# How the transposed operand of two large products leaves PSUM: split straight from PSUM, or scaled into SBUF first and split there

## The chip, the cores and the metric

The kernel runs on one core of a Trainium2 chip. The time is that of the device for one execution, in microseconds (us), as a median of repeated runs. The engines have the profile's names: PE multiplies and transposes, DVE and ACT work element by element, POOL does little here, and SP issues most of the transfers (DMA).

## What is computed

One layer of a streaming encoder with 256 tokens of width 4096, batch 1, all in fp32:

```python
xn = rms_norm(x, norm_in_g)
q, k, v, z_a, a_c, g_c, z_c = split(xn @ w_in)            # 4096 x 14336
y_a = rms_norm(chunked_attention(q, k, v, rel_table), attn_out_g) * silu(z_a)
y_c = rms_norm(conv_module(a_c, g_c, ...), conv_out_g) * silu(z_c)
h = x + concatenate([y_a, y_c]) @ w_out                    # 4096 x 4096, "the projection"
gate = sigmoid(rms_norm(h, ple_norm_g) @ w_ple_gate + b_ple_gate)   # 4096 x 4096, "the last gate"
h = h + gate * (p @ w_ple)                                 # 256 x 4096
return rms_norm(h, final_g)
```

## The kernel before

**Products.** Every fp32 product is made of three products of a shorter fp32 form (fp32r): each operand is split into a high part (the value rounded to that form) and a low part (the value minus its high part), and PE adds high·high, low·high and high·low. Weights come as blocks of 128 rows by 2 × 512 columns (tile `wt`, five buffers, loaded by SP at L440); ACT casts the high part (`wh`, L204) and DVE subtracts to get the low part (`wl`, L205), three buffers each.

**Pairs.** `mixed_product` takes the 32 blocks of 128 rows of the inner dimension in 16 pairs. A plain pair is 24 matmuls into four accumulator banks. A combined pair is 21 matmuls, by a scheme of seven products instead of eight: for it, DVE makes sums of the weights (`ua`, `ub`, L467 to L475) and sums of the other operand (`comb`), and four more PSUM banks hold partial results (`acc_P`). The order of the pairs is a string; the two products of the change begin with the order `late`, the eight odd pairs plain, and then 0 (combined), 2, 4 (combined) and so on.

**The operand.** `operand(src, g, c, ...)` makes chunk c, that is 512 of the 4096 inner rows (four blocks of 128), of the transposed left operand: PE transposes the activations into PSUM, 2 blocks to a bank (L170), and each block is scaled by a vector `g` on its way out. `split_from_psum` does that per block of 128 × 256: ACT writes the scaled high part (L156), and DVE reads PSUM again, scales and subtracts the high part (L157). For the combined pairs `combine` takes the first two blocks of a chunk: ACT writes the first block, scaled, into a row of SBUF (L284), DVE makes four sums of 128 columns in a second row, two of them reading the second block from PSUM (L268 to L271), and these 512 columns are split by ACT and DVE (L276, L277). The operand of the projection is `yT` (eight chunks, the last not combined here but later, by `combine_again`), that of the last gate `hT` (eight chunks, all combined). `y_ahead` and `h_ahead` call it one chunk ahead of the pair that uses it: chunks 0 and 1 at the last pair of the product before, then one for each odd pair. An odd pair uses the last two blocks of its chunk. After the eighth chunk of `hT`, `embedding` loads the layer's input embedding `p` into the tile `pin` (SP, L1113) and transposes it on PE.

**Buffers and order.** The rows of `combine`, the tile `pin` and the loaded rows of the gate's bias (L1002) share three buffers with the tag "row". PSUM has eight banks, four for accumulators (`acc`) and four for the rest. When one product ends and the next begins, the next takes over the accumulators as DVE empties them (L1067 for the gated columns before the projection, L1151 for h before the last gate). No order is written out by hand around the change: a list scheduler puts the instructions of the loops into each engine's queue, and each queue is worked through in order, SP's too.

Of the kernel before, what the change touches and what calls it, by code (L numbers as in the profile page):

```python
# [10 lines left out]
F32 = mybir.dt.float32  # L11
F32R = mybir.dt.float32r
AF = mybir.ActivationFunctionType
ALU = mybir.AluOpType
AX = mybir.AxisListType

P = 128
NB = 512
# [7 lines left out]
def hybrid_block(  # L26
# [23 lines left out]
    nc = tc.nc  # L50
    _, T, D = x.shape
# [16 lines left out]
    def pool(name, bufs, stack=ctx, side=0, **kw):  # L68
        return stack.enter_context(tc.tile_pool(name=name, bufs=bufs, side=sides[side], **kw))
# [12 lines left out]
    spool = pool("spool", 2, first_scratch, 1)  # L82
# [3 lines left out]
    def tmp_psum():  # L86
        return ps_tmp.tile([P, 512], F32, tag="tmp", name="tmp_ps")
# [61 lines left out]
    def big_tile(pool=None):  # L149
        return (pool or big).tile([P, 4, 2, T], F32R, tag="big", name="big_t")  # L150

    def split_from_psum(dst, i, src, scale):

        hi, lo = dst[:, i, 0, :], dst[:, i, 1, :]
        return (
            nc.scalar.activation(hi, src, AF.Identity, scale=scale),  # L156
            nc.vector.scalar_tensor_tensor(  # L157
                lo, src, scale, hi.bitcast(F32), ALU.mult, ALU.subtract
            ),
        )  # L160
# [3 lines left out]
    def transposed(src, blocks, then=lambda ins: None):  # L164

        pt = tmp_psum()
        for i, b in enumerate(blocks):
            for h in range(NH):
                last_transpose[:] = [
                    nc.tensor.transpose(  # L170
                        pt[:, i * T + h * P : i * T + (h + 1) * P],
                        src[:, h, b] if len(src.shape) == 4 else src[:, h, b * P : (b + 1) * P],
                        ident,
                    )
                ]
                then(*last_transpose)
        return [pt[:, i * T : (i + 1) * T] for i in range(len(blocks))]
# [80 lines left out]
    def sum_rows():  # L258
        return [spool.tile([P, NB], F32, tag="row", name="comb", bufs=3) for _ in range(2)]

    def combined_parts(dst, at, s, a, a01, a11, g, then=lambda ins: None):

        a00, a10 = a[:, :P], a[:, P:]
        s3, s5, s2, s4 = (s[:, i * P : (i + 1) * P] for i in range(4))
        stt = nc.vector.scalar_tensor_tensor
        then(nc.vector.tensor_tensor(s3, a00, a10, ALU.subtract))  # L268
        then(stt(s5, a11, g, a10, ALU.mult, ALU.subtract))
        then(stt(s2, s5, -1.0, a00, ALU.mult, ALU.subtract))  # L270
        then(stt(s4, a01, g, s2, ALU.mult, ALU.add))  # L271

        def split():
            hi, lo = dst[:, at : at + 2, 0, :], dst[:, at : at + 2, 1, :]
            src = s.rearrange("q (i t) -> q i t", t=T)
            then(nc.scalar.copy(hi, src))  # L276
            then(nc.vector.tensor_tensor(lo, src, hi.bitcast(F32), ALU.subtract))  # L277

        return split

    def combine(dst, at, pts, g):

        a, s = sum_rows()
        nc.scalar.activation(a[:, :T], pts[0], AF.Identity, scale=g[:, :1])  # L284
        combined_parts(dst, at, s, a[:, :T], pts[1][:, :P], pts[1][:, P:], g[:, 1:2])()

    def combine_again(dst, at, t, i, rows, then=lambda ins: None):

        a, s = rows
        then(  # L290
            nc.vector.tensor_tensor(
                a.rearrange("q (i t) -> q i t", t=T), t[:, i : i + 2, 0, :].bitcast(F32),
                t[:, i : i + 2, 1, :].bitcast(F32), ALU.add,
            )
        )
        return combined_parts(dst, at, s, a[:, :T], a[:, T : T + P], a[:, T + P :], 1.0, then)

    def comb_tile(combs, n_kept=0):

        if len(combs) < D // NB // 2 - 1 + n_kept:  # L300
            combs.append(big_tile(more))
        else:
            combs.append(keep.tile([P, 4, 2, T], F32R, tag="comb", name="comb_t"))

    def operand(src, g, c, tiles, combs, pool=None, combined=True):

        t = big_tile(pool)
        if c % 2 == 0:
            comb_tile(combs)
        for pair in range(2):  # L310
            blocks = (2 * pair, 2 * pair + 1)
            pts = transposed(src, blocks)
            for b, pt in zip(blocks, pts):
                split_from_psum(t, b, pt, g[:, b : b + 1])
            if pair == 0 and combined:
                combine(combs[c // 2], 2 * (c % 2), pts, g[:, :2])
        tiles.append(t)

    def pair_parts(src):
# [186 lines left out]
    tt, stt = nc.vector.tensor_tensor, nc.vector.scalar_tensor_tensor  # L506
# [53 lines left out]
    for c in range(0, 4, 2):  # L560
        if c:
            t = upool.tile([P, 4, 2, T], F32R, tag="big", name="big_t", bufs=1)
        else:
            t = keep.tile([P, 4, 2, T], F32R, tag="comb", name="comb_t")
# [3 lines left out]
    def combinations(c, then=lambda ins: None):  # L568

        rest = []  # L570

        def begin():
            rows = spool.tile([P, 2, NB], F32, tag="stage", name="comb")
            rest.append(
                combine_again(*xS[2 * c], xT[c], 0, (rows[:, 0], rows[:, 1]), then)
            )

        return begin, lambda: rest.pop()()

    def first_pairs(add):  # L580
# [62 lines left out]
        for n in range(1, n_x + 1):  # L643
# [26 lines left out]
    rows = [(conv_ln_g, KCW), (conv_ln_b, KCW), (b_dw, KCW), (attn_out_g, AW // P),  # L670
            (conv_out_g, KCW), (ple_norm_g, KD)]
    n_rows = sum(n for _, n in rows)
    at = [sum(n for _, n in rows[:i]) for i in range(len(rows))]
# [324 lines left out]
    def broadcast_row(src, n0, n, **kw):  # L998

        kw = kw or dict(tag="row", bufs=3)  # L1000
        t = spool.tile([P, n], F32, name="row", **kw)
        nc.sync.dma_start(  # L1002
            t, bass.AP(tensor=src.tensor, offset=src.offset + n0, ap=[[0, P], [1, n]])
        )
        return t
# [5 lines left out]
    for c in range(2):  # L1011
        uC[2 * c] = act.tile([P, 2, 2, T], F32R, tag="act", name="comb_u"), 0
        scratch = spool.tile([P, 2, NB], F32, tag="stage", name="comb")
        combine_again(*uC[2 * c], uS[c], 0, (scratch[:, 0], scratch[:, 1]))()
    first_scratch.close()
    spool = upool = pool("lpool", 2, side=1)
    y_c = []
    ssq_c = cpool.tile([P, NH, CW // NB], F32, name="ssq_c")
    for c0, order in zip(range(0, CW // NB, 2), point):
        row = broadcast_row(b_pw, c0 * NB, 2 * NB, tag="stage")  # L1020
        rows = [row[:, j * NB : (j + 1) * NB] for j in range(2)]
# [29 lines left out]
    for c in range(2, D // NB):  # L1051
        if c % 2 == 0:
            comb_tile(xS, 1)
        combine_again(xS[c // 2], 2 * (c % 2), xT[c], 0, sum_rows())()
# [24 lines left out]
    def y_ahead(pair):  # L1079
        while len(yT) < min(pair // 2 + 2, D // NB):  # L1080
            c = len(yT)
            if c == D // NB - 2:
                fill(len(later))
            y, g, at = (y_a[c], ga, 4 * c) if c < len(y_a) else (y_c[c - len(y_a)], gc, 4 * (c - len(y_a)))
            operand(
                y, g[:, at : at + 4], c, yT, yS, None if c else more, combined=c < D // NB - 1
            )
        if pair == late[9][0]:

            rest = []  # L1090
            later.append(
                lambda: rest.append(combine_again(yS[-1], 2, yT[-1], 0, sum_rows()))
            )
            later.append(lambda: rest.pop()())
# [23 lines left out]
    def h_ahead(pair):  # L1118
        while len(hT) < min(pair // 2 + 2, D // NB):
            c = len(hT)  # L1120
            operand(hs[c], gp[:, 4 * c : 4 * c + 4], c, hT, hS)
            if len(hT) == D // NB:
                embedding()

    ssq_h = cpool.tile([P, NH, D // NB], F32, name="ssq_h")
    for c0 in range(0, D // NB, 2):
        for j in range(2):
            hc = act.tile([P, NH, NB], F32, tag="act", name="hc")
            c = c0 + j
# [85 lines left out]
    rows, fgs = [], []  # L1215
# [51 lines left out]
    def sum_of(h, at):  # L1267
        s = end[:, 0, h : h + 1]
        pin(nc.vector.tensor_reduce(s, ssq_f[:, h, :at], AX.X, ALU.add))
        return s  # L1270
# [45 lines left out]
    s = sum_of(1, n_f + 1)  # L1316
# [35 lines left out]
```

## Time and profile before

| | |
|---|---|
| median of three runs | 2029.14 us (2028.86 to 2029.4) |
| profiled execution | 2028.23 us, span 2026.5 us |
| granted TensorE clock, mean | 0.998 |
| the projection's odd pairs (operand `yT`) | about 1307 to 1368 us of the span |
| the last gate's odd pairs (operand `hT`) | about 1644 to 1706 us of the span |

The profile is one execution. A row of a group gives the source line, the engine, the operation and its tiles, the number of instructions, their busy time in us, the mean of one in ns, and after the second bar the idle time of the engine just ahead of them with what ended it. A row of a timeline begins with the start and the duration in us. PEld is PE's weight load, which runs beside its matmuls; a wait of PE for an operand shows there. The name in front of the arrow is what is written.

### The profile page before, as it was taken

How to read it: one execution, taken by the hardware profiler on the slowest of the kernel's cores; microseconds unless marked ns; L12 is line 12 of the kernel's file. 1: busy time of each engine (PE TensorE's matmuls, PEld its weight loads, DVE VectorE, ACT ScalarE, POOL GpSimd, SP SyncE). 2: the span in 40 equal slices, each digit the busy share in tenths (PEclk: the TensorE clock that was granted, in tenths of full speed). 3: DMA queues.
4: the chain of work that ended last, by engine and by line, in shares of the span. 5: the costliest groups of instructions: out<-in, count | busy, mean ns of one | idle time of the engine just before them, and what ended most of it. 6: DMA issues, size and time to landing. Idle time of an engine off the chain costs nothing.

```text
span 2026.5 us, 26195 instructions
## 1 busy us (share of the span) xinstructions
PE 2010.8 (99%) x9073; PEld 1654.4 (82%) x9073; DVE 1903.4 (94%) x2708; ACT 1215.0 (60%) x1583; POOL 46.9 (2%) x50
## 2 busy tenths in 40 slices
PE   9999999999999999999999999999999999999997
PEld 7888888888888888788888888888888888888876
DVE  7999999889999997888899999999999999999998
ACT  7655545655655555776556556666665666655555
POOL 0000000000000000000000000000000000000000
PEclk9999999999999999999999999999999999999999
DMA  8787878678678867456666666676666656666765
GB/s 295 222 238 234 255 217 250 177 247 240 188 221 246 252 198 241 156 177 209 196 208 207 208 204 211 208 239 210 203 211 197 208 194 201 208 218 207 231 207 180
DMA packets 171168, 436.70 MB, mean 215 GB/s; under 512 B 13966, under 2 KB 17182, under 8 KB 171034
## 3 DMA queue, kind: packets, MB, share of 16 engines
q1 hardware_dynamic: 161952, 417.93, 63.9%
q0 software_dynamic: 8432, 16.25, 4.8%
q8 instruction: 71, 1.16, 0.2%
q10 hardware_dynamic: 650, 0.84, 0.1%
q14 instruction: 63, 0.52, 0.1%
HBM read 430.77 MB, written 4.19 MB: 215 GB/s over the span
## 4 chain that ended last, share of the span: by engine, by line
PE 95%; DVE 3%; issue 1%; ACT 1%; DMA 0%; POOLq 0%; POOL 0%; ACTq 0%; SPq 0%; DVEq 0%
PE acc L385 73%; PE acc_P L385 17%; PE tmp_ps L170 1%; DVE cv L724 1%; PE acc L229 1%; DVE wl L205 1%; PE tmp_ps L893 0%; PE tmp_ps L877 0%; PE tmp_ps L911 0%; PE tmp_ps L916 0%; PE acc L373 0%; ACT wh L204 0%; PE tmp_ps L892 0%; DVE ul L205 0%; DMA xin<-in_x_dram 0%
## 5 line engine op out<-in xcount | busy, mean ns | idle before, releaser
L385 PE MATMUL acc<-wh,big_t 128*128 128x512 f32 x4154 | 1283.3, 391 | 0.6 <-DVE y_c L1043 0.4
L204 ACT CAST wh<-wt 128x1024 fp32r<-128x1024 f32 (+1 forms) x737 | 710.1, 974 | 523.3 <-PE acc L385 364.3
L385 PEld LDWEIGHTS acc<-wh,big_t 128*128 128x128 f32 x4154 | 777.0, 188 | 160.8 <-DVE y_c L1043 0.9
L205 DVE TENSOR_TENSOR wl<-wt,wh 128x1024 fp32r<-128x1024 f32 (+1 forms) x737 | 817.4, 1122 | 39.9 <-ACT wh L204 33.6
L385 PE MATMUL acc<-wl,big_t 128*128 128x512 f32 x2077 | 801.9, 391 | 0.1
L385 PEld LDWEIGHTS acc<-wl,big_t 128*128 128x128 f32 x2077 | 389.5, 188 | 82.5 <-DVE wl L205 1.8
L204 ACT CAST uh<-ua 128x1024 fp32r<-128x1024 f32 x174 | 182.9, 1052 | 91.1 <-DVE ua L468 46.3
L205 DVE TENSOR_TENSOR ul<-ua,uh 128x1024 fp32r<-128x1024 f32 x174 | 212.0, 1219 | 9.6 <-ACT uh L204 8.1
L724 DVE SCALAR_TENSOR_TENSOR cv<-uT,dw,cv 128x250 f32<-128x250 f32 (+19 forms) x480 | 203.6, 464 | 1.1
L385 PE MATMUL acc_P<-uh,big_t 128*128 128x512 f32 x528 | 161.8, 392 | 0.0
L204 ACT CAST uh<-ub 128x1024 fp32r<-128x1024 f32 x92 | 96.8, 1052 | 95.5 <-DVE ub L475 79.2
L205 DVE TENSOR_TENSOR ul<-ub,uh 128x1024 fp32r<-128x1024 f32 x92 | 112.2, 1220 | 6.7 <-ACT uh L204 5.6
L385 PEld LDWEIGHTS acc_P<-uh,big_t 128*128 128x128 f32 x528 | 98.0, 188 | 23.2 <-ACT uh L204 3.7
L385 PE MATMUL acc_P<-ul,big_t 128*128 128x512 f32 x264 | 101.3, 392 | 0.0
L467 DVE TENSOR_TENSOR ua<-wt 128x512 f32<-128x512 f32 x102 | 69.9, 685 | 17.3 <-DMA wt<-in_w_in_dram 10.7
L385 PE MATMUL acc<-uh,big_t 128*128 128x512 f32 x266 | 82.5, 390 | 0.0
L385 PE MATMUL acc_P<-wh,big_t 128*128 128x512 f32 x266 | 82.1, 389 | 0.0
L468 DVE TENSOR_TENSOR ua<-wt 128x512 f32<-128x512 f32 x102 | 69.6, 683 | 4.3 <-DMA wt<-in_w_in_dram 3.6
L385 PE MATMUL acc_P<-uh,comb_t 128*128 128x512 f32 x228 | 70.1, 390 | 0.1
L475 DVE TENSOR_TENSOR ub<-ub,wt 128x512 f32<-128x512 f32 x92 | 63.0, 685 | 0.8
L474 DVE TENSOR_TENSOR ub<-ua,wt 128x512 f32<-128x512 f32 x92 | 62.9, 683 | 0.3
L385 PEld LDWEIGHTS acc_P<-ul,big_t 128*128 128x128 f32 x264 | 49.3, 188 | 12.5 <-DVE ul L205 2.0
(243 smaller groups left out, 1485.5 us busy)
## 6 DMA issues: line engine op xcount, KB each, us to landing
wt<-in_w_in_dram SPq DMA_DIRECT2D x416, 512.0 KB, 4.5
wt<-in_w_out_dram SPq DMA_DIRECT2D x128, 512.0 KB, 4.3
wt<-in_w_ple_gate_dram SPq DMA_DIRECT2D x128, 512.0 KB, 4.2
wt<-in_w_pw_dram SPq DMA_DIRECT2D x32, 512.0 KB, 4.8
ua<-in_w_in_dram SPq DMA_DIRECT2D x31, 512.0 KB, 4.3
ua<-in_w_in_dram POOLq DMA_DIRECT2D x31, 512.0 KB, 8.7
wt<-in_w_in_dram SPq DMA_DIRECT2D x31, 256.0 KB, 2.8
hc<-in_x_dram SPq DMA_DIRECT2D x8, 512.0 KB, 4.7
```

The source lines that it names most:

```text
L170: nc.tensor.transpose(pt[:, i * T + h * P : i * T + (h + 1) * P], src[:, h, b] if len(src.shape) == 4 else src[:, h, b * P : (b + 1) * P], ...
L204: nc.scalar.copy(wh[:, :kc, :], wt[:, :kc, :]),
L205: nc.vector.tensor_tensor(wl[:, :kc, :], wt[:, :kc, :], wh[:, :kc, :].bitcast(F32), ALU.subtract),
L229: nc.tensor.matmul(acc, a, b[:, k, :], start=kb == 0 and kind == 0, stop=kb == kblocks - 1 and kind == 2,)
L385: nc.tensor.matmul(banks[name], a, b, start=name not in begun, stop=final and ends[name] == n and kind == 2 and not (left and name in "P2 ...
L467: plus(ua[:, 0], w0[:, 0], w0[:, 1])
L468: plus(ua[:, 1], w0[:, 1], w1[:, 1])
L474: plus(ub[:, 0], ua[:, 0], w1[:, 1])
L475: plus(ub[:, 1], ub[:, 0], w1[:, 0])
L724: nc.vector.scalar_tensor_tensor(cv[:, i, PAD - k :], uT[:, i, : T + k - PAD], dw[:, b, k : k + 1], cv[:, i, PAD - k :], ALU.mult, ALU.add,)
```

## The change

`operand` now copies each transposed block, scaled by ACT, from PSUM into a row of fp32 in SBUF, two blocks to a row of 512 columns. Then one ACT cast of 512 columns makes both high parts, and one DVE subtraction of 512 columns, from SBUF, both low parts. `combine` takes its four quarters from that row, so its own copy L284 is gone and none of its sums reads PSUM or scales. A combined chunk therefore takes three rows of the tag "row" where it took two, and one that is not combined takes two where it took none. `combine_again` passes quarters too. The embedding still uses `split_from_psum`. The orders of the pairs and their products are the same.

```diff
     def sum_rows():
         return [spool.tile([P, NB], F32, tag="row", name="comb", bufs=3) for _ in range(2)]
 
-    def combined_parts(dst, at, s, a, a01, a11, g, then=lambda ins: None):
-        a00, a10 = a[:, :P], a[:, P:]
+    def combined_parts(dst, at, s, a00, a10, a01, a11, then=lambda ins: None):
         s3, s5, s2, s4 = (s[:, i * P : (i + 1) * P] for i in range(4))
         stt = nc.vector.scalar_tensor_tensor
         then(nc.vector.tensor_tensor(s3, a00, a10, ALU.subtract))
-        then(stt(s5, a11, g, a10, ALU.mult, ALU.subtract))
+        then(nc.vector.tensor_tensor(s5, a11, a10, ALU.subtract))
         then(stt(s2, s5, -1.0, a00, ALU.mult, ALU.subtract))
-        then(stt(s4, a01, g, s2, ALU.mult, ALU.add))
+        then(nc.vector.tensor_tensor(s4, a01, s2, ALU.add))
...
-    def combine(dst, at, pts, g):
-        a, s = sum_rows()
-        nc.scalar.activation(a[:, :T], pts[0], AF.Identity, scale=g[:, :1])
-        combined_parts(dst, at, s, a[:, :T], pts[1][:, :P], pts[1][:, P:], g[:, 1:2])()
+    def combine(dst, at, a):
+        s = spool.tile([P, NB], F32, tag="row", name="comb", bufs=3)
+        (a00, a10), (a01, a11) = ((a[:, i, :P], a[:, i, P:]) for i in range(2))
+        combined_parts(dst, at, s, a00, a10, a01, a11)()
...
-        return combined_parts(dst, at, s, a[:, :T], a[:, T : T + P], a[:, T + P :], 1.0, then)
+        return combined_parts(dst, at, s, *(a[:, i * P : (i + 1) * P] for i in range(4)), then)
...
     def operand(src, g, c, tiles, combs, pool=None, combined=True):
         t = big_tile(pool)
         if c % 2 == 0:
             comb_tile(combs)
+        rows = sum_rows()
         for pair in range(2):
             blocks = (2 * pair, 2 * pair + 1)
-            pts = transposed(src, blocks)
-            for b, pt in zip(blocks, pts):
-                split_from_psum(t, b, pt, g[:, b : b + 1])
+            a = rows[pair].rearrange("q (i t) -> q i t", t=T)
+            for i, pt in enumerate(transposed(src, blocks)):
+                b = blocks[i]
+                nc.scalar.activation(a[:, i], pt, AF.Identity, scale=g[:, b : b + 1])
+            hi, lo = (t[:, 2 * pair : 2 * pair + 2, q, :] for q in range(2))
+            nc.scalar.copy(hi, a)
+            nc.vector.tensor_tensor(lo, a, hi.bitcast(F32), ALU.subtract)
             if pair == 0 and combined:
-                combine(combs[c // 2], 2 * (c % 2), pts, g[:, :2])
+                combine(combs[c // 2], 2 * (c % 2), a)
         tiles.append(t)
```

In the changed file the copies are L315, the cast of a row L317, the low part of a row L318; the sums of `combined_parts` are L267 to L270 and its split L275 and L276; `combine_again` adds at L290; matmuls are L389, weight loads L444, the sums of weights L471 to L479, the emptying of accumulators L1071 and L1155, the row loads L1006 and the load of `pin` L1117.

## The prediction

> **What bounds the kernel now.** I read the page first (busy time, then the chain that ended last), then the windows of the two stages in which the changed routine runs, then the waits of PE's weight loads after them. The columns of the page's first line are busy us, share of the span and instructions; those of a window are its length, then busy us of PE, PEld, DVE, ACT and POOL with instruction counts, the granted clock, the DMA share and GB/s.
>
> ```profile
> PE 2010.8 (99%) x9073; PEld 1654.4 (82%) x9073; DVE 1903.4 (94%) x2708; ACT 1215.0 (60%) x1583; POOL 46.9 (2%) x50
> PE 95%; DVE 3%; issue 1%; ACT 1%; DMA 0%; POOLq 0%; POOL 0%; ACTq 0%; SPq 0%; DVEq 0%
> 1300.00:1370.00 70.00, 70.00 (x342) 58.42 (x341) 64.59 (x115) 46.85 (x76) 0.00 (x0) 1.00 0.70 232
> 1640.00:1710.00 70.00, 70.00 (x344) 58.58 (x343) 66.22 (x121) 48.98 (x85) 0.69 (x1) 1.00 0.59 191
> PEld acc_P L385 <- ACT uh L204: 4.5, 16, 0.5
> PEld acc_P L385 <- DVE ul L205: 1.3, 6, 0.3
> PEld acc L385 <- DVE wl L205: 0.9, 3, 0.3
> PEld acc L373 <- DVE big_t L205: 0.5, 1, 0.5
> ```
>
> PE carries 95% of the chain. In both windows of the change it is busy for all 70 us at clock 1.00: **there is no wait of PE there to remove**, so a lighter DVE or a heavier ACT is worth nothing unless PE is made to wait, and every such wait is lost for good. The last four rows are all the waits of PE's loads from 1720 to 2000 us, 7.2 us in sum; only from there could a gain come.
>
> **The routine itself.** Groups by line: count, busy us, mean ns, idle before and its releaser.
>
> ```profile
> L156 ACT ACTIVATE big_t<-tmp_ps,prm 128x256 fp32r<-128x256 f32 x64 | 27.7, 470 | 4.1 <-DVE big_t L157 2.5 <-PE tmp_ps L170 1.6
> L157 DVE SCALAR_TENSOR_TENSOR big_t<-tmp_ps,prm,big_t 128x256 fp32r<-128x256 f32 x64 | 28.2, 476 | 0.0
> L276 ACT CAST big_t<-comb 128x512 fp32r<-128x512 f32 x20 | 12.0, 615 | 2.6 <-DVE comb L271 2.2 <-issue 0.3
> L277 DVE TENSOR_TENSOR big_t<-comb,big_t 128x512 fp32r<-128x512 f32 x20 | 13.5, 686 | 1.6 <-ACT big_t L276 1.6
> L284 ACT ACTIVATE comb<-tmp_ps,prm 128x256 f32<-128x256 f32 x15 | 7.1, 470 | 0.0
> L268 DVE TENSOR_TENSOR comb<-comb 128x128 f32<-128x128 f32 x30 | 8.6, 287 | 0.9 <-ACT comb L284 0.7
> L269 DVE SCALAR_TENSOR_TENSOR comb<-tmp_ps,prm,comb 128x128 f32<-128x128 f32 x15 | 5.2, 343 | 0.0
> L270 DVE SCALAR_TENSOR_TENSOR comb<-comb 128x128 f32<-128x128 f32 x30 | 8.5, 284 | 0.1
> L271 DVE SCALAR_TENSOR_TENSOR comb<-tmp_ps,prm,comb 128x128 f32<-128x128 f32 x15 | 5.2, 344 | 0.0
> L205 DVE TENSOR_TENSOR wl<-wt,wh 128x1024 fp32r<-128x1024 f32 (+1 forms) x737 | 817.4, 1122 | 39.9 <-ACT wh L204 33.6
> ```
>
> A combined chunk on ACT: before 4 × 470 + 470 + 615 = 2965 ns. After: the four copies still read PSUM in 256 columns (470 each, the nearest row for the new output type), the extra copy L284 goes, two casts of 512 columns come (615 each): 1880 + 1230 + 615 = 3725 ns, **+0.76 us**. On DVE: before 4 × 476 + 287 + 343 + 284 + 344 + 686 = 3848 ns. After: two subtractions of 512 columns (686, the row of the same form), and four sums of 128 columns all from SBUF (287, 287, 284, 287): 1372 + 1145 + 686 = 3203 ns, **−0.645 us**. The page's fifteen combined chunks (x15) make ACT +11.4 and DVE −9.7 us; the one that is not combined adds 1230 ns on ACT and takes 532 on DVE. ACT has some 21 of 70 us idle in each window and DVE 4 to 5, so neither sum reaches PE. In `combine_again` one form replaces another at the same 287 against 286 to 290: nothing. PE's and POOL's instructions are the same in number. So the price lies only in order and buffers, at five places.
>
> **First, the start of the projection.** PE, from the last matmuls of the previous product (acc_10871) into the new one (acc_11620 on), before and after:
>
> ```order
> L385 MATMUL acc_10871<-wh,big_t 128x512 x2
> L385 MATMUL acc_10871<-wl,big_t 128x512
> L385 MATMUL acc_11620<-wh,big_t 128x512 x2
> L385 MATMUL acc_11620<-wl,big_t 128x512
> L385 MATMUL acc_11620<-wh,big_t 128x512 x2
> L170 MATMUL tmp_ps<-ident,qT 128x128 x11
> L385 MATMUL acc_11622<-wh,big_t 128x512 x2
> ```
> ```order
> L389 MATMUL acc_10871<-wh,big_t 128x512 x2
> L389 MATMUL acc_10871<-wl,big_t 128x512
> L389 MATMUL acc_11620<-wh,big_t 128x512 x2
> L389 MATMUL acc_11620<-wl,big_t 128x512
> L389 MATMUL acc_11622<-wh,big_t 128x512 x2
> L389 MATMUL acc_11622<-wl,big_t 128x512
> L389 MATMUL acc_11620<-wh,big_t 128x512 x2
> L389 MATMUL acc_11621<-wh,big_t 128x512 x2
> ```
>
> The eleven transposes that gave DVE time to empty the old accumulators have left this place. What they cover in the trace (start, us, engine, line; the bracket is idle time and releaser):
>
> ```profile
> 1314.91 0.62 PE L385 MATMUL acc<-wh,big_t 128*128 128x512 f32 x2
> 1316.05 1.36 PE L170 MATMUL tmp_ps<-ident,qT 128*128 128x128 f32 x11
> 1313.90 0.34 DVE L271 SCALAR_TENSOR_TENSOR comb<-tmp_ps,prm,comb 128x128 f32<-128x128 f32 x1
> 1316.16 1.28 DVE L1067 TENSOR_TENSOR z<-acc,z 128x512 f32<-128x512 f32 x2
> 1317.70 0.69 DVE L277 TENSOR_TENSOR big_t<-comb,big_t 128x512 fp32r<-128x512 f32 x1 [0.26 <-ACT big_t L276]
> 1652.87 1.36 PE L170 MATMUL tmp_ps<-ident,hc 128*128 128x128 f32 x11
> 1654.52 0.69 DVE L277 TENSOR_TENSOR big_t<-comb,big_t 128x512 fp32r<-128x512 f32 x1 [0.30 <-ACT big_t L276]
> ```
>
> Five matmuls take 1316.05 − 1314.91 = 1.14 us, 0.227 each. After, PE asks for the third old bank 8 matmuls past 1314.91, at 1316.7. DVE's list after puts one short sum, an emptying, a low part (L318), a combined split (L276) and only then the third emptying: from 1313.90 on 0.2 + 4 × 0.6 = 2.6 us, plus the 0.26 that L277 waits for ACT here, makes 1316.8; the fourth comes two steps later, with its bank wanted 0.7 after the third. I take **+0.45** (0 to 1.2: to 1317.4, the end of the trace's pair of emptyings, and a late cast). The last gate starts in the same way (1652.87, 1654.52): **+0.5** (0 to 1.2).
>
> **Second, the end of the projection's odd pairs.** DVE, where chunk 7 (big_t_11987) is made and the weights of the first combined pair (wt_12078, after wt_12080) are summed, before and after:
>
> ```order
> L467 TENSOR_TENSOR ua_12090<-wt_12078 128x512
> L271 SCALAR_TENSOR_TENSOR comb_11934<-tmp_ps_11924,prm_125,comb_11934 128x128
> L157 SCALAR_TENSOR_TENSOR big_t_11987<-tmp_ps_11988,prm_125,big_t_11987 128x256
> L157 SCALAR_TENSOR_TENSOR big_t_11987<-tmp_ps_11997,prm_125,big_t_11987 128x256
> L277 TENSOR_TENSOR comb_t_11923<-comb_11934,comb_t_11923 128x2x256
> L157 SCALAR_TENSOR_TENSOR big_t_11987<-tmp_ps_11988,prm_125,big_t_11987 128x256
> L157 SCALAR_TENSOR_TENSOR big_t_11987<-tmp_ps_11997,prm_125,big_t_11987 128x256
> ```
> ```order
> L471 TENSOR_TENSOR ua_12092<-wt_12080 128x512
> L270 TENSOR_TENSOR comb_11935<-comb_11924,comb_11935 128x128
> L318 TENSOR_TENSOR big_t_11922<-comb_11925,big_t_11922 128x2x256
> L205 TENSOR_TENSOR wl_12029<-wt_12010,wh_12028 128x1024
> L276 TENSOR_TENSOR comb_t_11923<-comb_11935,comb_t_11923 128x2x256
> L472 TENSOR_TENSOR ua_12092<-wt_12080,wt_12082 128x512
> L478 TENSOR_TENSOR ub_12103<-ua_12092,wt_12082 128x512
> L205 TENSOR_TENSOR wl_12049<-wt_12044,wh_12048 128x1024
> L479 TENSOR_TENSOR ub_12103<-ub_12103,wt_12082 128x512
> L318 TENSOR_TENSOR big_t_11987<-comb_11988,big_t_11987 128x2x256
> L290 TENSOR_TENSOR comb_12167<-big_t_11987 128x512
> L205 TENSOR_TENSOR ul_12096<-ua_12092,uh_12095 128x1024
> ```
>
> The row after these is the second L318 of big_t_11987, which pair 15 needs. The sum that waits for a transfer now stands twelve rows ahead of it, not six.
>
> ```profile
> 1347.51 4.71 SPq L440 DMA_DIRECT2D wt<-in_w_out_dram  x3
> 1352.26 1.04 PE L170 MATMUL tmp_ps<-ident,y_c 128*128 128x128 f32 x8
> 1354.15 0.69 DVE L467 TENSOR_TENSOR ua<-wt 128x512 f32<-128x512 f32 x1 [1.23 <-DMA wt<-in_w_out_dram]
> 1359.45 0.69 DVE L468 TENSOR_TENSOR ua<-wt 128x512 f32<-128x512 f32 x1
> 1360.06 0.69 DVE L474 TENSOR_TENSOR ub<-ua,wt 128x512 f32<-128x512 f32 x1
> ```
>
> In a row, 512 columns take 0.61 us (1359.45 to 1360.06), 1024 some 1.13. From the start of L471 to the end of that L318 are 9 × 0.6 + 3 × 1.13 + 0.2 = 9.0. Chunk 7's transposes end at about 1353.2 and one pair of 24 matmuls (5.44) later, at 1358.6, PE begins pair 15; with the 0.45 above, 1359.1. So L471 must start by 1350.1. I estimate that DVE reaches it at 1349.4 to 1350, one chunk (6.4 us) after the same place of the chunk before. The transfer took 6.6 us here (1347.51 to 1354.15), issued behind an hc load; after, it stands ahead of that load and its buffer comes free some 2 us sooner. By those 6.6 it lands near 1352: PE waits some 2; if it lands in time, nothing. I take **+1.4** (0 to 2.9, a landing at 1353).
>
> **Third, the end of the last gate's odd pairs.** SP loads the embedding's input `pin`, which shares the three buffers of tag "row"; each chunk now takes three of them, not two. The view is DVE's list, before and after; the tiles comb_14907 and comb_14918 belong to chunk 6, comb_14982 and comb_14985 to chunk 7.
>
> ```order
> L277 TENSOR_TENSOR comb_t_14907<-comb_14918,comb_t_14907 128x2x256
> L157 SCALAR_TENSOR_TENSOR big_t_14971<-tmp_ps_14972,prm_125,big_t_14971 128x256
> L157 SCALAR_TENSOR_TENSOR big_t_14971<-tmp_ps_14990,prm_125,big_t_14971 128x256
> L205 TENSOR_TENSOR wl_15068<-wt_15049,wh_15067 128x1024
> L268 TENSOR_TENSOR comb_14982<-comb_14981 128x128
> ```
> ```order
> L267 TENSOR_TENSOR comb_14985<-comb_14974 128x128
> L268 TENSOR_TENSOR comb_14985<-comb_14974 128x128
> L205 TENSOR_TENSOR ul_15101<-ua_15097,uh_15100 128x1024
> L318 TENSOR_TENSOR big_t_14973<-comb_14974,big_t_14973 128x2x256
> L269 SCALAR_TENSOR_TENSOR comb_14985<-comb_14985,comb_14974 128x128
> L479 TENSOR_TENSOR ub_15108<-ub_15108,wt_15087 128x512
> L270 TENSOR_TENSOR comb_14985<-comb_14974,comb_14985 128x128
> ```
>
> Before, `pin` waits for the first row above (L277 of chunk 6); after, its buffer is comb_14974's, so it waits for the last row, L270 of chunk 7.
>
> ```profile
> 1689.74 0.27 PE L170 MATMUL tmp_ps<-ident,hc 128*128 128x128 f32 x1
> 1692.36 0.69 DVE L277 TENSOR_TENSOR comb_t<-comb,comb_t 128x512 fp32r<-128x512 f32 x1
> 1693.08 0.38 SPq L1113 DMA_DIRECT2D pin<-in_p_dram  x1
> 1697.84 0.60 PE L170 MATMUL tmp_ps<-ident,pin 128*128 128x128 f32 x4
> pin<-in_p_dram SPq DMA_DIRECT2D x1, 256.0 KB, 3.9
> ```
>
> Issued at 1693.08, it landed at 1697.0, 0.8 before PE used it. After: chunk 7's last transpose ends near 1690.0, or 1690.5 with the 0.5 above; two copies on ACT (0.8) and the seven rows (0.2 + 0.2 + 1.13 + 0.6 + 0.2 + 0.6 + 0.2 = 3.1) give 1694.4 at the earliest, and 1695.7 with a weight cast (1.05) ahead of them. I take 1695.7, since both engines are full there: landing 1699.6, asked for near 1697.85, **+1.75** (0.45 to 1.75 by those two). The Trainium skill, "SBUF — State Buffer", section "The DMA setup-cost knee", gives a transfer about 2 us plus its bytes at 436 GB/s; an estimate from that page is 2.6 us for this one, a wait of 0.45 and a sum of 3.6. The trace disagrees with 3.9, and I use the trace. The second low part of chunk 7 adds **+0.4** (0 to 0.9).
>
> **Fourth, the first combined pairs of the last gate.** The rows' loads and the sum L471 of the next combined pair move ahead of two wide subtractions on DVE; a like wait for weights in the trace is 1.43 us:
>
> ```profile
> 1730.77 0.69 DVE L513 TENSOR_TENSOR z<-acc_P,z 128x512 f32<-128x512 f32 x1 [0.37 <-PE acc_P L385]
> 1740.33 0.69 DVE L467 TENSOR_TENSOR ua<-wt 128x512 f32<-128x512 f32 x1 [1.43 <-DMA wt<-in_w_ple_gate_dram]
> ```
>
> I take +0.4 (0 to 1.4). Sum: 0.45 + 1.4 + 0.5 + 1.75 + 0.4 + 0.4 = **+4.9 us**. The profiled execution took 2028.23 (span 2026.5), 0.91 below the median 2029.14; so 2033.1 for such a run and **2034.0** as median.
>
> **The rivals.** *Hidden:* transfers land in time, only the two starts and a rest cost: +1 to +2.5, 2030 to 2031.6. For it: 0.8 us of room at `pin`, and a late wait that is only estimated. *Larger:* every term at its upper end (1.2 + 2.9 + 1.2 + 1.75 + 0.9 + 1.4 = 9.35); some 7 of it, 2036 to 2038, if the transfers collide. *Faster:* DVE's 9.7 us and ACT's freedom become a lead that shortens the 7.2 us of PE waits after 1720; it decides when over 4.1 of those go and the starts cost nothing: about 2025. Against it: DVE waits for PE at 1730.77 and for weights at 1740.33, so a lead is spent there. Its other source is the 2.5 us that ACT waits for DVE at L156: they share a PSUM bank before, and not after. The Trainium skill, "PSUM — Partial Sum Buffer", section "PSUM bank collisions raise a hardware error ⚠️", says that the compiler makes any two engines on one bank take turns. By that rule, the trace agrees (2.5 us), and all of it regained would be 2026.6; but PE waits for none of it in the window.
>
> **How the numbers follow.** Forecast 0.55, larger 0.22, hidden 0.14, faster 0.09. 0.2% is 4.06 us, about what a measurement of this kernel can tell from no change. The forecast's own spread (the sum with `pin` at 0.45 and the second place at 0 is 2.2; with both starts at 1.2 and that place at 2.9, 7.9) lies above 4.06 for 0.42 of its 0.55. Slower 0.42 + 0.22 = 0.64, same 0.13 + 0.14 = 0.27, faster 0.09. The range leaves out faster and the extremes: 2029.8 to 2038.0.
>
> **What would show it.** Right: PE idle near 1316, 1358, 1653 and before `pin`'s transposes, each with a DVE or DMA releaser; `pin` issued near 1695 to 1697; ACT's 256-column copies no longer waiting for DVE. Wrong: PE busy throughout both windows (then hidden), or fewer than 3 us of waits after 1720 (then faster).

## The result and the profile after

The changed kernel takes 2031.2 us (median of 22 runs, 2029.91 to 2033.9), the kernel before 2028.84 in the same comparison (22 runs, 2027.7 to 2030.59). The ratio is 1.0013, with a 95% interval of 1.0007 to 1.0019: 1.4 to 3.9 us slower, below the 0.2% that the prediction drew as its line. The profiled execution took 2033.1 us (span 2031.3), 1.9 above its median, so its own difference of 4.9 us to the profiled execution of before is twice what the medians show; a second profile of the changed kernel (below) has a span of 2030.0.

The page of the changed kernel, busy times and the chain that ended last:

```profile
PE 2013.3 (99%) x9073; PEld 1653.8 (81%) x9073; DVE 1898.0 (93%) x2676; ACT 1226.5 (60%) x1600; POOL 47.6 (2%) x50
PE 89%; DVE 6%; issue 2%; DMA 1%; ACT 1%; POOLq 0%; POOL 0%; ACTq 0%; DVEq 0%; SPq 0%
```

ACT is busy 11.5 us more and DVE 5.4 less. PE's part of the chain falls from 95% to 89%: work of other engines now stands between matmuls. The groups of the new lines:

```profile
L315 ACT ACTIVATE comb<-tmp_ps,prm 128x256 f32<-128x256 f32 x64 | 27.0, 469 | 0.0
L318 DVE TENSOR_TENSOR big_t<-comb,big_t 128x512 fp32r<-128x512 f32 x32 | 21.9, 685 | 0.4 <-ACT big_t L317 0.2
L317 ACT CAST big_t<-comb 128x512 fp32r<-128x512 f32 x32 | 19.9, 623 | 0.8
L270 DVE TENSOR_TENSOR comb<-comb 128x128 f32<-128x128 f32 x30 | 8.6, 287 | 0.5
```

The durations are those of the prediction's nearest rows (470, 686, 615, 287), and ACT's copies out of PSUM no longer wait: 0.0 of idle time ahead of them where L156 had 4.1, 2.5 of it for DVE. Yet the projection's part, and the last gate's, now hold waits of PE's weight loads. First the waits of the changed kernel from 1300 to 1400, then those from 1640 to 1720 us (in sum, times, longest):

```profile
PEld acc L389 <- DVE big_t L318: 1.0, 1, 1.0
PEld acc L389 <- DVE z L1071: 0.7, 2, 0.4
PEld acc L389 <- DVE wl L205: 0.5, 1, 0.5
PEld acc_P L389 <- DVE ul L205: 0.2, 1, 0.2
...
PEld acc L389 <- DVE wl L205: 0.9, 1, 0.9
PEld tmp_ps L170 <- issue: 0.7, 1, 0.7
PEld acc L389 <- DVE hc L1155: 0.7, 2, 0.4
```

Before, there was 0.2 in the first window (for `ul`) and nothing in the second. The waits for `wl` and `ul` come behind the odd pairs (1366 to 1400 and 1704 to 1720); the other places are those that the order had shown. The timeline of the changed kernel (loads of PE, DVE, SP, PE):

```profile
1317.50 0.30 PEld L389 LDWEIGHTS acc<-wh,big_t 128*128 128x128 f32 x2 [0.41 <-DVE z L1071]
1318.74 0.30 PEld L389 LDWEIGHTS acc<-wh,big_t 128*128 128x128 f32 x2 [0.25 <-DVE z L1071]
1350.12 0.68 DVE L471 TENSOR_TENSOR ua<-wt 128x512 f32<-128x512 f32 x1
1354.17 0.69 DVE L472 TENSOR_TENSOR ua<-wt 128x512 f32<-128x512 f32 x1 [0.82 <-DMA wt<-in_w_out_dram]
1359.58 0.68 DVE L318 TENSOR_TENSOR big_t<-comb,big_t 128x512 fp32r<-128x512 f32 x1
1360.32 0.19 PEld L389 LDWEIGHTS acc<-wh,big_t 128*128 128x128 f32 x1 [0.97 <-DVE big_t L318]
1696.59 0.28 DVE L270 TENSOR_TENSOR comb<-comb 128x128 f32<-128x128 f32 x1
1696.94 0.38 SPq L1117 DMA_DIRECT2D pin<-in_p_dram  x1
1699.72 0.63 PE L170 MATMUL tmp_ps<-ident,pin 128*128 128x128 f32 x4 [0.33 <-DMA pin<-in_p_dram]
```

The third row to the sixth are one story: the sum L471 starts on time, the next sum waits 0.82 us for its weights, and seven rows further in DVE's list the low part that pair 15 needs ends at 1360.26, with PE's load 0.97 us late. The last three rows are the other: `pin` is issued within 0.1 us of the end of chunk 7's sum, as its shared buffer demands, and PE's transposes wait for it.

**Two stretches as a measure.** The 22 runs of before lie within 2.9 us and those of the changed kernel within 4.0, more than what is to be explained. Two stretches can be compared more sharply: from the first transposes of the operand (`yT`, `hT`) to the first matmul of a combined pair (`acc_P`). In every kernel here each holds the same 216 matmuls, and 64 transposes at the projection, 68 at the last gate. Before and after, from the timeline of PE:

```profile
1307.71 1.91 PE L170 MATMUL tmp_ps<-ident,qT 128*128 128x128 f32 x16
1364.06 0.62 PE L385 MATMUL acc_P<-wh,big_t 128*128 128x512 f32 x2
1644.50 1.91 PE L170 MATMUL tmp_ps<-ident,hc 128*128 128x128 f32 x16
1701.26 0.62 PE L385 MATMUL acc_P<-wh,big_t 128*128 128x512 f32 x2
```

```profile
1308.33 1.91 PE L170 MATMUL tmp_ps<-ident,qT 128*128 128x128 f32 x16
1365.67 0.61 PE L389 MATMUL acc_P<-wh,big_t 128*128 128x512 f32 x2
1646.33 1.91 PE L170 MATMUL tmp_ps<-ident,hc 128*128 128x128 f32 x16
1703.85 0.62 PE L389 MATMUL acc_P<-wh,big_t 128*128 128x512 f32 x2
```

Before: 1364.06 − 1307.71 = 56.35 and 1701.26 − 1644.50 = 56.76 us. After: 57.34 and 57.52, so +0.99 and +0.76. The table has the same differences for every run, each from one profile; the last column is the time against the kernel before, as a ratio with its interval where it was timed.

| kernel | projection | last gate | ratio |
|---|---|---|---|
| before | 56.35 | 56.76 | |
| before_copy | 56.35 | 56.76 | |
| the changed kernel | 57.34 | 57.52 | 1.0013 (1.0007 to 1.0019) |
| after_again | 57.12 | 57.63 | 1.0011 (1.0003 to 1.0020) |
| hold | 56.50 | 58.41 | 1.0011 (1.0003 to 1.0020) |
| pin_own | 57.11 | 57.00 | 1.0006 (0.9997 to 1.0015) |
| hold_pin | 56.49 | 56.98 | 1.0009 (1.0000 to 1.0018) |
| late_one | 56.47 | 56.91 | 1.0007 (0.9998 to 1.0016) |
| y_only | 57.33 | 56.68 | 1.0003 (0.9994 to 1.0012) |
| h_only | 56.35 | 57.59 | 1.0005 (0.9996 to 1.0014) |
| part_split | 56.93 | 58.86 | |
| part_comb | 56.12 | 56.61 | |
| part_comb_timed | 56.16 | 56.61 | 1.0002 (0.9993 to 1.0011) |
| act_twice | 57.06 | 57.29 | |

### The profile page after: what moved, and what is told of

Its sections match the earlier page's. It is cut to its first block, busy times and chain, and to the rows that moved or that the text cites. A ratio compares the mean times of both kernels' runs of the same rounds, so it can differ in the third digit from the quotient of the medians.

```text
span 2031.3 us, 26204 instructions
## 1 busy us (share of the span) xinstructions
PE 2013.3 (99%) x9073; PEld 1653.8 (81%) x9073; DVE 1898.0 (93%) x2676; ACT 1226.5 (60%) x1600; POOL 47.6 (2%) x50
## 4 chain that ended last, share of the span: by engine, by line
PE 89%; DVE 6%; issue 2%; DMA 1%; ACT 1%; POOLq 0%; POOL 0%; ACTq 0%; DVEq 0%; SPq 0%
PE acc L389 69%; PE acc_P L389 17%; DVE wl L205 2%; DVE cv L728 1%; PE tmp_ps L170 1%; DVE ul L205 1%; DMA wt<-in_w_out_dram 1%; PE acc L229 1%; DMA wt<-in_w_ple_gate_dram 1%; PE tmp_ps L897 0%; PE tmp_ps L881 0%; PE tmp_ps L915 0%; ACT wh L204 0%; DVE cv L806 0%; PE tmp_ps L920 0%
## 5 line engine op out<-in xcount | busy, mean ns | idle before, releaser
L389 PE MATMUL acc<-wh,big_t 128*128 128x512 f32 x4154 | 1286.4, 391 | 1.6 <-ACT big_t L156 0.7
L389 PEld LDWEIGHTS acc<-wh,big_t 128*128 128x128 f32 x4154 | 776.8, 188 | 163.0 <-ACT big_t L156 1.5
L389 PE MATMUL acc<-wl,big_t 128*128 128x512 f32 x2077 | 804.7, 392 | 0.9 <-DVE wl L205 0.6
L389 PEld LDWEIGHTS acc<-wl,big_t 128*128 128x128 f32 x2077 | 389.6, 188 | 84.9 <-DVE wl L205 4.5
L389 PE MATMUL acc_P<-uh,big_t 128*128 128x512 f32 x528 | 161.9, 392 | 0.5 <-ACT uh L204 0.4
L389 PEld LDWEIGHTS acc_P<-uh,big_t 128*128 128x128 f32 x528 | 98.0, 188 | 23.6 <-ACT uh L204 4.1
L389 PE MATMUL acc_P<-ul,big_t 128*128 128x512 f32 x264 | 101.4, 392 | 0.1
L471 DVE TENSOR_TENSOR ua<-wt 128x512 f32<-128x512 f32 x102 | 70.0, 686 | 24.9 <-DMA wt<-in_w_in_dram 14.1
L389 PE MATMUL acc<-uh,big_t 128*128 128x512 f32 x266 | 82.6, 390 | 0.0
L389 PE MATMUL acc_P<-wh,big_t 128*128 128x512 f32 x266 | 82.1, 389 | 0.0
L472 DVE TENSOR_TENSOR ua<-wt 128x512 f32<-128x512 f32 x102 | 69.7, 683 | 3.5 <-DMA wt<-in_w_in_dram 1.3
L389 PE MATMUL acc_P<-uh,comb_t 128*128 128x512 f32 x228 | 70.1, 390 | 0.1
L479 DVE TENSOR_TENSOR ub<-ub,wt 128x512 f32<-128x512 f32 x92 | 63.0, 685 | 0.8
L389 PEld LDWEIGHTS acc_P<-ul,big_t 128*128 128x128 f32 x264 | 49.3, 188 | 12.8 <-DVE ul L205 2.5
```

Source lines behind the costliest of these rows:

```text
L389: nc.tensor.matmul(banks[name], a, b, start=name not in begun, stop=final and ends[name] == n and kind == 2 and not (left and name in "P2 ...
L471: plus(ua[:, 0], w0[:, 0], w0[:, 1])
L472: plus(ua[:, 1], w0[:, 1], w1[:, 1])
L479: plus(ub[:, 1], ub[:, 0], w1[:, 0])
```

## The experiments

The theory: the change costs where it moves instructions and buffers, at the two starts, at the sum that waits for weights ahead of the last low part, and at `pin`. The rival: the heavier ACT, or the way through SBUF itself, costs.

**Both kernels again.** First the kernel before.

> The kernel before once more, for a second profile: by how much its stretches vary from run to run. Both theories: the stretch from the projection's first transposes to its first combined matmul (56.35 us in the first profile) and the one of the last gate (56.76) within 0.1, since no transfer ends a wait there; the stretches outside (1307.7 us before, 325.2 after) may move by up to 1 us.

Its stretches are the same to 0.01 us, while the span (2026.2 against 2026.5) moved by 0.3. So differences of 0.1 in the table mean something where no transfer ends a wait. Then the changed kernel.

> The changed kernel once more, for its profile and as the reference of this group. Theory (order and buffers): 2 to 3.5 us above the kernel before; waits of PE's loads near 1317, 1360, 1655, before pin's transposes, and in the first combined pairs of the last gate (1706 to 1722). What differs from profile to profile should be the waits that a transfer ends, not those at the two starts. Rival (the heavier ACT): the same total, but with ACT as releaser of PE's waits in the two windows.

2031.32 us, against 2029.52 for before. The waits at the starts came back to the tenth, those that a transfer ends were 0.7 where they had been 1.0 (L318), and 0.9 where they had been 0.7 (`pin`). ACT is the releaser of none of them. By these waits the stretches differ from the first profile's, by 0.22 and 0.11: where a transfer ends a wait, no smaller difference in the table can be read.

**Which product.** The old operand is used for one of the two; this is the edit of `y_only`, and `h_only` has the same at the call for `yT`:

```diff
-            operand(hs[c], gp[:, 4 * c : 4 * c + 4], c, hT, hS)
+            operand_old(hs[c], gp[:, 4 * c : 4 * c + 4], c, hT, hS)
```

> The new operand for the projection alone; the last gate has the old one. Theory (order and buffers): its stretch at the projection as in the changed kernel (57.1 to 57.4 us, 0.8 to 1 over before), the last gate's stretch as before (56.8), the rest as before: 0.6 to 1.4 us above before in all. Rival (ACT's load): the same sign, half of the total, but with ACT as releaser.

> The new operand for the last gate alone. Theory: the projection's stretch as before (56.35), the last gate's 57.5 to 57.6 (0.8 over before, 0.6 of it by pin), and some 0.5 us after it in the first combined pairs: 1 to 2 us above before. Rival (what is lost comes from the projection): 0 to 0.5 us.

The stretches did as expected: the one with the new operand costs what it costs in the changed kernel (57.33; 57.59), the other is as before (56.68; 56.35). In whole runs 2030.14 and 2030.13 against 2029.23: +0.9 each by the medians, though neither interval excludes 0. The 0.5 us behind the last gate's stretch that `h_only` was expected to show is not there (its 2028.3 − 1703.25 = 325.05 us, before 2026.5 − 1701.26 = 325.24).

**The sums held back.** The sums of a combined pair in the order `late` are issued after the parts of the pair ahead:

```diff
-                plus(ua[:, 0], w0[:, 0], w0[:, 1])
-                plus(ua[:, 1], w0[:, 1], w1[:, 1])
+                with queued_behind(before if order is late else ()):
+                    plus(ua[:, 0], w0[:, 0], w0[:, 1])
+                    plus(ua[:, 1], w0[:, 1], w1[:, 1])
```

> The changed kernel, with the first sums of weights (L471, L472) of each combined pair in the two products of the order late held back until the parts of the pair before are issued. Theory: the wait at the end of the projection's odd pairs (about 1.5 us in the profile of the changed kernel) and part of the 2 us in the last gate's first combined pairs go: 0.5 to 1.5 us above before. Rival (the 12 us more on ACT or the lighter DVE cost the time, wherever the sums stand): 2 to 3.5 us above before, as the changed kernel.

The waits of PE's loads in `hold`, from 1300 to 1400 and then from 1640 to 1810 the first row of the view:

```profile
PEld acc L389 <- DVE z L1072: 0.7, 2, 0.4
PEld acc_P L389 <- DVE ul L205: 0.6, 1, 0.6
...
PEld tmp_ps L170 <- issue: 1.7, 1, 1.7
```

The wait for L318 is gone, and the projection's stretch falls from 57.12 to 56.50 (57.34 in the first profile): the sum's place cost 0.6 to 0.8 us there. The wait of 0.6 for `ul` comes behind the stretch, between 1380 and 1400, so that the sums held back give some of the gain up again. The total did not fall (2031.6, 2.1 above before, where 0.5 to 1.5 was expected): in the last gate the same edit moved `pin`'s transposes earlier, to 50.8 us into the stretch from 52.7, and they now wait 1.7 us (58.41).

**`pin` in another buffer.**

```diff
-        pin = spool.tile([P, NH, PLE], F32, tag="row", name="pin", bufs=3)
+        pin = spool.tile([P, 2, NB], F32, tag="stage", name="pin")[:, 0].rearrange("q (h n) -> q h n", n=PLE)
```

> The changed kernel, with the embedding's input pin in a buffer of the tag stage, which is free well before, instead of a row. Theory: pin is issued several us earlier and the 0.7 to 0.9 us wait before its transposes goes, and SP's queue behind it moves up, which may also take some of the waits at 1706 to 1722: 0.8 to 2.3 us above before. Rival (pin was hidden, or its time comes back at the next wait): as the changed kernel, 2 to 3.5 us above.

All that is left of waits from 1640 to 1706 in `pin_own` is the start:

```profile
PEld acc L389 <- DVE hc L1155: 0.7, 2, 0.4
```

The stretch falls from 57.63 (57.52 in the first profile) to 57.00, the time to 2030.44 (before 2029.52). So the shared buffer cost 0.5 to 0.6 us.

> Both edits together. Theory: only the two starts are left (0.7 us of waits each in the profile, some 0.5 each on PE): 0.3 to 1.2 us above before. Rival (heavier ACT): still 2 to 3.5 us above.

Both stretches add up as expected (56.49, 56.98), 0.14 and 0.22 above before, which is what is left for the starts. The whole run does not show it: 2030.79, by the medians 1.3 above before, with an interval of 0 to 0.18%.

**The starts.** On top of `hold_pin`, only chunk 0 is made at the last pair of the product before, so that DVE's list has two instructions between the four emptyings, where it had four.

```diff
-        return lambda pair: make(0) if pair == dense[-1][0] else None
+        return lambda pair: make(-2) if pair == dense[-1][0] else None
```

> The changed kernel with the held sums, pin in a buffer of its own, and only chunk 0 (not 0 and 1) made at the last pair of the product before, so that DVE empties the old accumulators sooner. Theory: the two waits of 0.7 us for the old accumulators go, both stretches come to those of before or 0.1 to 0.3 below (56.1 to 56.4, 56.5 to 56.8): within 0.5 us of before in all. Rival (ACT and the third pass over SBUF hold PE back): 0.7 to 2 us above before, as with the two edits alone. Risk: chunk 1 comes late for pair 3, a new wait of up to 1 us near 1320.

Its waits from 1300 to 1400, and from 1640 to 1705:

```profile
PEld acc L389 <- DVE big_t L318: 0.4, 1, 0.4
PEld acc_P L389 <- DVE ul L205: 0.4, 1, 0.4
...
PEld acc L389 <- DVE big_t L318: 0.4, 1, 0.4
```

The waits for the old accumulators are gone, as meant, and chunk 1's low part is late instead, as feared: 56.47 and 56.91, a gain of 0.02 and 0.07. At 2031.0 us, 1.8 above before (2029.23) where at most 0.5 was expected, the edit brought nothing.

**One part at a time.** `part_split` has the row, the wide cast and the wide low part, and combines from PSUM. `part_comb` splits from PSUM as before and combines from a scaled copy:

```diff
             for b, pt in zip(blocks, pts):
                 split_from_psum(t, b, pt, g[:, b : b + 1])
             if pair == 0 and combined:
-                combine(combs[c // 2], 2 * (c % 2), pts, g[:, :2])
+                row = spool.tile([P, NB], F32, tag="row", name="comb", bufs=3)
+                a = row.rearrange("q (i t) -> q i t", t=T)
+                for b, pt in zip(blocks, pts):
+                    nc.scalar.activation(a[:, b], pt, AF.Identity, scale=g[:, b : b + 1])
+                combine(combs[c // 2], 2 * (c % 2), a)
```

> One part of the change alone: the row in SBUF, one cast and one low part of 512 columns, while the combination still reads the second block from PSUM and scales it (four DVE sums as before). Three rows per chunk, as in the change. Theory (order and buffers): stretches of the changed kernel, the projection's 57.0 to 57.4 us (before 56.35) and the last gate's 57.4 to 57.7 (before 56.76), pin issued only after chunk 7's sums. Rival (what costs is the combination from SBUF): both as before, within 0.2.

> The other part alone: blocks are split from PSUM in 256 columns as before, and ACT copies the first two blocks of a chunk, scaled, into a row from which the combination takes its quarters. Two rows per chunk, as before, and 470 ns more on ACT for each chunk. Theory: pin comes in time, since its buffer is free after chunk 6, the first sums stand behind the low parts: both stretches within 0.3 us of before (56.35 and 56.76). Rival (any shift of work to ACT costs): 0.5 to 1 us more in each.

The waits of `part_split` from 1640 to 1706, and the only one of `part_comb` in either stretch of its first profile:

```profile
PEld tmp_ps L170 <- issue: 2.2, 1, 2.2
PEld acc L410 <- ACT comb L333: 0.4, 1, 0.4
```

```profile
PEld acc L388 <- DVE wl L205: 0.2, 1, 0.2
```

The wide split with three rows per chunk carries the cost: +0.58 and +2.10, where the changed kernel has 0.8 to 1.0 and 0.8 to 0.9. PE waits 0.6 for the low part at the end of the projection's odd pairs and 2.2 for `pin`, which makes the last gate's stretch longer than expected; at the starts it waits for ACT's copies (0.4), not for the old accumulators. The combination from SBUF carries no cost and is 0.23 and 0.15 under before, though ACT has 470 ns more per combined chunk. Timed:

> The combination from a scaled copy in SBUF, low parts from PSUM as before, now timed. Its one profile had both stretches 0.23 and 0.15 us below before (56.12, 56.61) and no wait in them. Theory: 0.4 us below before in the two stretches, so between 1 us below and 1 us above in all, since the rest varies by as much from run to run; clearly below the changed kernel's 2 us. Rival (its gain in the stretches is lost behind them): 1 to 2 us above before.

2029.86 us against 2029.51: no difference. The 0.4 us of the two stretches, found in both profiles, cannot be told from the rest of a run.

**ACT's load.** On `hold_pin`, the cast of each row is issued twice.

```diff
             nc.scalar.copy(hi, a)
+            nc.scalar.copy(hi, a)
```

> The changed kernel with held sums and pin in its own buffer, and the cast of each row (615 ns) issued twice, with the same result: 1.23 us more on ACT for each of the 16 chunks, 10 us in each stretch. Theory (ACT has some 12 us idle in each stretch, so its load is free): the stretches stay at 56.5 and 57.0, within 0.3. Rival (ACT's load is what costs): they grow by 1 us or more each, in proportion to the 6 us that the change added.

Its windows (length, then busy PE, PEld, DVE, ACT, POOL):

```profile
1306.00:1370.00 64.00, 63.96 (x313) 52.69 (x312) 57.33 (x92) 57.25 (x99) 0.00 (x0) 1.00 0.71 231
1645.00:1712.00 67.00, 66.90 (x329) 55.38 (x328) 60.25 (x99) 58.95 (x107) 0.69 (x1) 1.00 0.58 185
```

ACT is busy 57.25 of 64 us and 58.95 of 67, where `hold_pin` has 51.69 and 52.99: 5.6 and 6.0 us more, and not the 10 expected (sixteen casts; neighbours overlap, and other casts moved out). The change itself put 7.7 and 3.6 us on ACT in these windows (44.31 to 52.04, 48.21 to 51.85 in the first profiles). The stretches grow by 0.57 and 0.31 (57.06, 57.29): more than the 0.3 that I expected in the first, and less than the 1 us that the rival asked for. PE lost it at two low parts that came late (L319, the line L318 of the changed kernel):

```profile
1355.07 0.19 PEld L390 LDWEIGHTS acc<-wh,big_t 128*128 128x128 f32 x1 [0.48 <-DVE big_t L319]
1667.44 0.19 PEld L390 LDWEIGHTS acc<-wh,big_t 128*128 128x128 f32 x1 [0.53 <-DVE big_t L319]
```

Just ahead of each, DVE had waited 0.78 and 0.69 us for a weight cast of ACT. The doubled cast also moved the order, so the load alone may be less than this; it is not wholly free on an ACT that is already at 52 of 64. The stronger evidence against the rival is `hold_pin` itself: its ACT is as busy as in the changed kernel, and 0.14 and 0.22 us are left.

## Why the prediction held, and where its terms were off

The direction and the mechanism were right, the size was twice too large: +4.9 us forecast, +2.4 measured by the medians (1.4 to 3.9). The range held it, but the range was wide, from 0.7 to 8.9 us above before. By the line of 0.2% the outcome was the one given 0.27, not the slower one given 0.64. The time itself, 2031.2, lies where the rival *hidden* had it (2030 to 2031.6), though not for that rival's reason: transfers did end waits, at the end of the projection's odd pairs and at `pin`, for less than the forecast had. And it was luck that the profiled execution came out 4.8 us of span above before, close to 4.9: only 1.75 of it lies in the two stretches and 0.95 in the last place of the sum; 1.3 comes behind that, and 0.8 ahead of and between the stretches.

**What bounds the kernel.** Right. The steady chunks have no wait in either stretch. The saving on DVE was smaller than the sum of the means (10.2 with the chunk that is not combined, 5.4 measured): neighbours overlap, two L157 in a row took 0.87 us in before and not 0.95, so that fewer and wider instructions save less than their means. That had no consequence, and PE's waits behind 1720 did not shrink (8.3 us from 1720 to 2000 in the first profile, 7.2 before): no lead was carried on, and *faster* fell as argued.

**The starts**, +0.45 and +0.5, measured 0.14 and 0.22 to 0.24 against before. The waits of the loads are there (0.41 + 0.25 us), but PE lost less, as its own timeline in the changed kernel shows:

```profile
1316.89 1.33 PE L389 MATMUL acc<-wh,big_t 128*128 128x512 f32 x4
1318.06 0.40 PE L389 MATMUL acc<-wl,big_t 128*128 128x512 f32 x1
1318.30 1.18 PE L389 MATMUL acc<-wh,big_t 128*128 128x512 f32 x4
1319.32 0.40 PE L389 MATMUL acc<-wl,big_t 128*128 128x512 f32 x1
```

Nine matmuls from 1316.89 to 1319.32 take 2.43 us, nine of 0.227 would take 2.04: 0.39 lost. That is close to `hold` against `part_comb`, whose stretch has no such wait (56.50 − 56.12 = 0.38). Against before it is only 0.14, since before is 0.23 over `part_comb` itself. Why was not isolated: before has nine separate groups of transposes there, `part_comb` eight and the changed kernel seven.

**The end of the projection's odd pairs**, +1.4, measured 0.6 to 0.85 (`hold` against both profiles). The failed step is the landing of the first weights near 1352: DVE did not wait for them at all, and started L471 at 1350.12, 41.8 us after the stretch's first transposes, where the prediction's limit was 42.4 (1350.1 − 1307.71). The wait came one sum later, 0.82 at L472. Without that wait the list from L471 to the low part took 9.3 us, near the 9.0 of the prediction.

**`pin`**, +1.75 with +0.4 for the low part, measured 0.5 to 0.6 in all. The term itself has two slips: 1694.4 and a cast of 1.05 make 1695.45, not 1695.7, and the 0.5 of the start was added to the time of issue but not to the 1697.85 at which PE asks. Without them the same rows give 1.0. Counted from the stretch's first transposes, it was issued 50.6 us in (before 48.6), 2.0 later where the prediction had 2.6; and it landed after 2.6 us in this profile, 2.8 in the second, where the row of before had 3.9. In the fourteen profiles the same load took 2.6 to 4.4 us (4.4 in `part_split`, with its wait of 2.2). One landing was taken for a constant. The estimate of 2.6 us that the prediction worked out from the Trainium skill, "SBUF — State Buffer", section "The DMA setup-cost knee", and set aside for the row, is the lower end of what the runs show, 2.6 to 4.4.

The spread does not look like chance: it goes with the weight load of 512 KB that SP issued just ahead of `pin`. The rows of these loads, in before and in the changed kernel:

```profile
1684.91 7.93 SPq L440 DMA_DIRECT2D wt<-in_w_ple_gate_dram  x3
1687.06 7.01 SPq L444 DMA_DIRECT2D wt<-in_w_ple_gate_dram  x3
```

Before, the issue of the last of the three ended 0.24 us ahead of `pin`'s at 1693.08; in the changed kernel it ended 2.87 us ahead of `pin`'s at 1696.94. Counted from start to start, the five profiles with 0.6 us between that load and `pin` took 3.8 to 4.0 us to land `pin`, the seven with 3.1 to 3.2 took 2.6 to 2.8, and `hold` and `part_split`, with 1.6 and 1.7, took 3.7 and 4.4. So by making `pin` later the change seems to have made its landing shorter as well; no run isolates this.

No separate cost of the low part was seen once `pin` was out of the way (56.98 is before plus the start).

**The first combined pairs of the last gate**, +0.4: in the first profile of the change DVE waits 2.35 us for weights at L471, ahead of a product's low part,

```profile
1714.18 0.69 DVE L471 TENSOR_TENSOR ua<-wt 128x512 f32<-128x512 f32 x1 [2.35 <-DMA wt<-in_w_ple_gate_dram]
```

and the next product (L229, the first matmul of p · w_ple) starts 41.75 us after the first `acc_P`, not 40.80 as before. In the second profile, in `h_only` and in `pin_own` it is 40.80 again: 0 or 0.95, by how a transfer falls. Behind that place the runs differ once more: from the first L229 to the end are 284.4 us before, 285.7 and 284.9 in the two profiles of the change. The wait of 1.43 us that before has at 1740.33 is 2.68 in the first of them, but 2.48 in `y_only` too, whose last gate has the old operand and whose end is as late (285.7):

```profile
1745.35 0.69 DVE L471 TENSOR_TENSOR ua<-wt 128x512 f32<-128x512 f32 x1 [2.68 <-DMA wt<-in_w_ple_gate_dram]
1742.78 0.69 DVE L506 TENSOR_TENSOR ua<-wt 128x512 f32<-128x512 f32 x1 [2.48 <-DMA wt<-in_w_ple_gate_dram]
```

So a difference of this size comes without the new operand.

The two stretches give 1.6 to 1.8 us, and the first combined pairs of the last gate up to 0.95. The medians differ by 1.8 and 2.4, with intervals of 0.6 to 4.1 and 1.4 to 3.9. What the rest of the run adds, if anything, stays open: the time ahead of the projection's first transposes was 1307.7 and 1307.9 in the two profiles of before and 1307.9 to 1310.2 in the others, in code whose instructions there are nearly the same.

## What to carry to other kernels

Where one engine is busy all the time, moving work between two engines that have room is worth nothing in itself; look instead at what the edit does to the order in each queue and to shared buffers, at the first and the last turn of a loop above all. A load that shares a ring of buffers with a loop inherits the loop's last release: give it a buffer that is free earlier. And size a wait that a transfer ends by several landings in the trace, not by one, and look at what was issued just ahead of each, since the edit can change that too; compare stretches with the same instructions when whole runs vary by more than the effect.

## What the runs showed that was not expected

- The same stretch of 216 matmuls and 64 transposes took 56.12 us in `part_comb`, with 0.2 us of waits, and 56.35, twice, in the kernel before, whose loads show no wait in it. Why is open.
- With ACT busy 57.25 of 64 us, where before has 44.31, the projection's stretch is only 0.7 us longer (56.35 to 57.06), starts included.
- One load of 256 KB took between 2.6 and 4.4 us from issue to landing in fourteen profiles, in step with what had been issued just ahead of it.
